# A third Strassen-like group of seven products in five blocks of each FFN, sums written over their own weights, and another order at the borders

## The chip, the core and the metric

The kernel runs on one core of a Trainium2 chip. The metric is the device time of one execution in microseconds. TensorE (PE) multiplies, PEld loads its stationary operand, VectorE (DVE) does elementwise work on two tensors, ScalarE (ACT) copies, scales and evaluates functions, SyncE (SP) issues nearly all DMAs. Each engine takes its own instructions in order and waits on semaphores for the others.

## What is computed

One decoder layer on 256 tokens of width 2048, all in float32:

```python
h = h + 0.5 * rms_norm(swiglu(rms_norm(h, pre1), gate1, up1, down1), post1)     # FFN 1, D_FF = 5632
h = h + rms_norm(hybrid_mixer(rms_norm(h, preM), ...) @ w_out, postM)           # GLA and MoBA heads
h = h + 0.5 * rms_norm(swiglu(rms_norm(h, pre2), gate2, up2, down2), post2)     # FFN 2
def swiglu(h, w_gate, w_up, w_down): return (silu(h @ w_gate) * (h @ w_up)) @ w_down
```

The weights are 352.67 MB, read once; each is used for 256 tokens, in two halves t of 128.

## The kernel before

**Precision.** A float32 product is made of three: every operand is split into a high part (rounded to fp32r) and a low part (the rest), and hi x hi, hi x lo and lo x hi are added in PSUM. Weights arrive in half MBs (`raw`, 128 x 1024: two k-tiles by 512 columns). `split` makes `whi` on ACT (L133) and `wlo` on DVE (L134). A ring of `RING = 8` pairs (hi, lo) stands between them and PE, and a ring of `RAW = 5` raw halves between the loads and the split. Each ordinary half is used by 12 matmuls of 512 columns (`mmt`, L320 to L322): two k-tiles, two token halves, three products.

**Order.** The weights' order is planned first (`plan...`, list `forms`). `take` hands the next split pair to PE, `done` gives it back, and both call `ahead`, which writes out loads while fewer than 5 raw halves are held and splits while fewer than 8 pairs are. Tile's scheduler then sets the order of each engine's instructions: ready work may be moved ahead of work that is written earlier but waits. On the chip that order is fixed.

**FFN.** 11 blocks of 512 gate and 512 up columns: blocks 0 and 1 plain (`up`, `columns`), blocks 2 to 10 mixed (`unit`). After block 2, half a down group (8 halves, `down`) stands before each mixed block; then come groups 4 and 5, the last in `down_last`. A mixed block treats the two token halves and two halves of a part of k as a 2 x 2 block matrix, as it does gate and up, and makes seven products for eight (`product`, L510 to L512, 6 matmuls each). One "group" ("q") covers four halves of weights (w11 and w12 of gate and up, w22, w21) and needs seven split pieces: w11, t1, t3, w22, t2, w21, t4, where t1 = w11 + w12, t2 = t1 + w22, t3 = w12 + w22 and t4 = t2 + w21 are sums on DVE (L139, L171) into a tile of their own. The rest of k goes as ordinary halves ("s"), 4 between and 4 after the two groups. The input's mixtures, the left-hand sides, are made once per FFN by `mixed`, in steps between the products of blocks 0 and 1; `NQ` is the number of k pieces it provides for. After the last group of a block L541 to L545 add the products' results from PSUM, after its last ordinary halves L556 to L561 make silu(gate) x up, and `turned` (L594, L595) transposes and splits the result for `down`.

**Borders.** `down_last` finishes a sub-layer. It goes through the token halves t and in each through four groups of 512 columns: L394 adds the PSUM result to the earlier sum in `f`, L395 squares it on ACT with a running sum, L396 multiplies by the post-norm weight. Two groups share one PSUM tile (`pt`, 4 buffers of two banks each). `Late` continues: `after` makes the row norm (`rstd_tok`, L265 to L267, then `refined`, L255 to L258), `update` adds to h (L432) and squares the new h (L433) for the next norm, `chunk` transposes h (L443) and splits it into `xh`, the next sub-layer's input (L450 on ACT, L451 on DVE), between the first products of the next block in `columns`. `warm` has ACT load the table for the square root. The end of the kernel uses `write_out` (L628) in place of `Late`.

Of the kernel before, what the change touches and what calls it, by code (L numbers as in the profile page):

```python
# [10 lines left out]
F32 = mybir.dt.float32  # L11
# [6 lines left out]
P = 128  # L18
# [19 lines left out]
NQ = 2  # L38
# [15 lines left out]
UNIT = [("q", 0), ("s", 4), ("s", 12), ("s", 5), ("s", 13), ("q", 1), ("s", 6), ("s", 14), ("s", 7), ("s", 15)]  # L54
# [3 lines left out]
def layer(ctx, tc, xT, x, wn, wpo, cst, msk, bdec, wup, wglr, gu1, dn1, win, wo, gu2, dn2, out):  # L58
# [29 lines left out]
    def plan_up(gu, b):  # L88
# [5 lines left out]
        for kind, i in UNIT:  # L94
# [19 lines left out]
    raws, ready, sums = [], [], []  # L114
    read, used, freed = [0], [0], [0]
    sum_pool = [None]
# [20 lines left out]
    def added(name, a, b):  # L137
        t = sum_pool[0].tile([P, 1024], F32, name=name, tag="sum", bufs=2)
        V.tensor_tensor(t, a, b, ALU.add)  # L139
        sums.append(t)  # L140


    NEEDS = {"w": 1, "w11": 2, "t1": 3, "t3": 3, "w22": 3, "t2": 3, "w21": 4, "t4": 4}
    ENDS = {"w": 1, "w11": 1, "t1": 1, "t3": 2, "w22": 3, "t2": 3, "w21": 4, "t4": 4}

    def can_prep():
# [4 lines left out]
        return len(raws) >= r + NEEDS[kind] and (kind[0] != "t" and kind != "w11" or sum_pool[0] is not None)  # L151

    def prep(cuts=1):
        kind, r = forms[len(ready)]
        w = raws[r:r + 4]
        if kind == "w" or kind == "w11":
            if kind == "w11":
                added("t1", w[0], w[1])
            split(w[0], cuts)
        elif kind == "t1":  # L160
            added("t2", sums[-1], w[2])
            split(sums[-2])
        elif kind == "t3":
            added("t3", w[1], w[2])
            split(sums[-1])
        elif kind == "w22":
            split(w[2])
        elif kind == "t2":
            split(sums[-2])
        elif kind == "w21":  # L170
            V.tensor_tensor(sums[-2], sums[-2], w[3], ALU.add)  # L171
            split(w[3])
        else:
            split(sums[-2])
# [155 lines left out]
    def columns(p, late=None):  # L330
# [3 lines left out]
        if late is not None:  # L334
            lead = []
            for t in range(NT):
# [3 lines left out]
                for i in range(LEAD):  # L340
# [36 lines left out]
    def down_last(g, lhs, wpost, sq, late):  # L377
# [4 lines left out]
        warm(eps)  # L382
        slots = []
        for t in range(NT):
            for m in range(4):
                if m % 2 == 0:
                    pair = pt()
                p = pair[:, m % 2]
# [4 lines left out]
                d = f[:, m, t]  # L393
# [628 lines left out]
```

## Time and profile before

| | |
|---|---|
| time, median of 3 runs | 1860.88 us (1860.2 to 1861.45) |
| the profiled execution | 1861.03 us, span 1859.2 us |
| granted TensorE clock, mean | 0.996 |
| PE, PEld, DVE, ACT busy | 98%, 82%, 77%, 54% |
| matmuls | 8516 |
| read from HBM | 352.67 MB, 191 GB/s over the span |

FFN 1 takes the span up to about 705 us, the mixer up to about 1122, FFN 2 the rest. A matmul's recorded duration is longer than the time until the next one starts, since they are pipelined; the starts tell the rate. The same holds for DVE and ACT to a smaller degree.

### The profile page before, as it was taken

To read this page: it belongs to the slowest core of one execution; us is meant where nothing else is said; L and a number is where in the kernel's file an instruction comes from. 1 tells how busy PE (TensorE), PEld (TensorE's weight loads), DVE (VectorE), ACT (ScalarE), POOL (GpSimd) and SP (SyncE) were. 2 spreads that over 40 slices of the span, in tenths; PEclk is the share of its full clock that TensorE was granted. 3 is DMA by queue.
4 is the path that set the end of the run, shared out by engine and by line. 5 is a ranking of instruction groups with operands and counts; after the bars stand their busy time and mean duration, and the time that the engine had idled before them with its cause. 6 is when DMAs were issued, how large, how long until landed. Compare 5 with 4: busy or idle time off the path is not lost.

```text
span 1859.2 us, 22693 instructions
## 1 busy us (share of the span) xinstructions
PE 1830.4 (98%) x8516; PEld 1518.6 (82%) x8516; DVE 1428.9 (77%) x1568; ACT 999.8 (54%) x1191; POOL 0.2 (0%) x4
## 2 busy tenths in 40 slices
PE   8999999999999998999999998999999999999997
PEld 6888888888888886889888886888888888888886
DVE  6788888888888857568455648778888888888875
ACT  7555555455545546454445547545564555455552
POOL 0000000000000000000000000000000000000000
PEclk9999999999999999999999999999999999999999
DMA  8664666556555763644355553645665565556571
GB/s 331 215 215 159 200 221 211 172 192 228 192 191 194 247 206 111 231 150 142 131 169 171 200 184 110 221 168 193 226 202 177 198 227 174 201 203 215 171 249 67
DMA packets 99086, 356.27 MB, mean 192 GB/s; under 512 B 11136, under 2 KB 11392, under 8 KB 98720
## 3 DMA queue, kind: packets, MB, share of 16 engines
q1 hardware_dynamic: 98400, 353.77, 56.9%
q8 instruction: 67, 1.10, 0.2%
q10 hardware_dynamic: 576, 1.05, 0.2%
q14 instruction: 43, 0.35, 0.1%
HBM read 352.67 MB, written 2.10 MB: 191 GB/s over the span
## 4 chain that ended last, share of the span: by engine, by line
PE 97%; ACT 1%; DVE 1%; DMA 0%; issue 0%; DVEq 0%; SPq 0%; ACTq 0%
PE pt L320 22%; PE pt L321 22%; PE pt L322 22%; PE pt L308 6%; PE pt L510 6%; PE pt L511 6%; PE pt L512 6%; PE pt L309 3%; PE pt L588 1%; PE pt L804 1%; ACT whi L133 1%; DVE h L628 0%; DVE wlo L134 0%; ACT f L433 0%; DVE f L394 0%
## 5 line engine op out<-in xcount | busy, mean ns | idle before, releaser
L134 DVE TENSOR_TENSOR wlo<-raw,whi 128x1024 fp32r<-128x1024 f32 (+1 forms) x621 | 755.6, 1220 | 235.7 <-ACT whi L133 218.7
L133 ACT ACTIVATE whi<-raw 128x1024 fp32r<-128x1024 f32 (+1 forms) x621 | 655.6, 1058 | 474.9 <-PE pt L322 306.4
L320 PE MATMUL pt<-whi,xh 128*128 128x512 f32 x1088 | 429.1, 395 | 13.3 <-ACT whi L133 6.2
L322 PE MATMUL pt<-whi,xh 128*128 128x512 f32 x1088 | 425.6, 392 | 1.0 <-DVE rt_v L267 0.6
L321 PE MATMUL pt<-wlo,xh 128*128 128x512 f32 x1088 | 426.1, 392 | 0.0
L133 ACT ACTIVATE whi<-t 128x1024 fp32r<-128x1024 f32 x144 | 152.3, 1057 | 258.6 <-DVE t L139 155.0
L320 PE MATMUL pt<-whi,act 128*128 128x512 f32 x704 | 276.6, 393 | 3.7 <-DVE f L394 3.6
L321 PE MATMUL pt<-wlo,act 128*128 128x512 f32 x704 | 274.7, 390 | 0.0
L322 PE MATMUL pt<-whi,act 128*128 128x512 f32 x704 | 274.5, 390 | 0.0
L320 PEld LDWEIGHTS pt<-whi,xh 128*128 128x128 f32 x1088 | 205.2, 189 | 61.7 <-ACT xh L450 10.4
L322 PEld LDWEIGHTS pt<-whi,xh 128*128 128x128 f32 x1088 | 205.2, 189 | 46.6 <-DVE xh L451 2.5
L321 PEld LDWEIGHTS pt<-wlo,xh 128*128 128x128 f32 x1088 | 205.2, 189 | 42.0 <-DVE wlo L134 0.9
L134 DVE TENSOR_TENSOR wlo<-t,whi 128x1024 fp32r<-128x1024 f32 x144 | 176.1, 1223 | 80.4 <-ACT whi L133 79.8
L308 PE MATMUL pt<-xh,whi 128*128 128x512 f32 x512 | 181.9, 399 | 0.0
L320 PEld LDWEIGHTS pt<-whi,act 128*128 128x128 f32 x704 | 132.6, 188 | 32.9 <-DVE f L394 5.3
L322 PEld LDWEIGHTS pt<-whi,act 128*128 128x128 f32 x704 | 132.6, 188 | 27.7
L321 PEld LDWEIGHTS pt<-wlo,act 128*128 128x128 f32 x704 | 132.6, 188 | 26.8
L309 PE MATMUL pt<-xh,wlo 128*128 128x256 f32 x512 | 143.7, 281 | 0.0
L139 DVE TENSOR_TENSOR t<-raw 128x1024 f32<-128x1024 f32 x72 | 88.1, 1224 | 42.2 <-DMA raw<-in_gu 41.0
L308 PEld LDWEIGHTS pt<-xh,whi 128*128 128x128 f32 x512 | 96.1, 188 | 22.6 <-issue 0.8
L510 PE MATMUL pt<-whi,mix 128*128 128x512 f32 x288 | 112.0, 389 | 0.0
L511 PE MATMUL pt<-wlo,mix 128*128 128x512 f32 x288 | 112.0, 389 | 0.0
(175 smaller groups left out, 1618.7 us busy)
## 6 DMA issues: line engine op xcount, KB each, us to landing
raw<-in_gu SPq DMA_DIRECT2D x351, 512.0 KB, 4.0
raw<-in_dn SPq DMA_DIRECT2D x176, 512.0 KB, 4.6
raw<-in_win SPq DMA_DIRECT2D x96, 512.0 KB, 3.4
raw<-in_wo SPq DMA_DIRECT2D x32, 512.0 KB, 3.3
wpost<-in_wpo SPq DMA_DIRECT2D x6, 512.0 KB, 6.2
hT<-in_xT SPq DMA_DIRECT2D x8, 256.0 KB, 7.0
h<-in_x SPq DMA_DIRECT2D x2, 1024.0 KB, 9.4
out<-h SPq DMA_DIRECT2D x4, 256.0 KB, 2.6
```

The costliest lines, as they stand in the source:

```text
L133: A.activation(hi[:, c], w[:, c], AF.Copy)
L134: V.tensor_tensor(lo[:, c], w[:, c], hi[:, c].bitcast(F32), ALU.subtract)
L139: V.tensor_tensor(t, a, b, ALU.add)
L308: T.matmul(o, hv[:, k, c], a, start=first and k == 0, stop=False)
L309: T.matmul(o[:, S:], lv[:, k, c], a[:, 0:S], start=False, stop=last and k == 1)
L320: T.matmul(o, hi, hv[:, i], start=first and i == 0, stop=False)
L321: T.matmul(o, hi, lv[:, i], start=False, stop=False)
L322: T.matmul(o, lo, hv[:, i], start=False, stop=last and i == 1)
L510: T.matmul(o, a[:, 0], hv[:, i], start=first and i == 0, stop=False)
L511: T.matmul(o, a[:, 0], lv[:, i], start=False, stop=False)
L512: T.matmul(o, a[:, 1], hv[:, i], start=False, stop=last and i == 1)
L588: T.transpose(p[:, j // 2, j % 2 * S + t * P:j % 2 * S + (t + 1) * P], s[:, t, j * P:(j + 1) * P], ident)
```

## The change

- `NQ` becomes 3, and a mixed block has one of two orders: blocks 3, 5, 7, 9 and 10 three groups and 4 ordinary halves (2 after the first group, 2 at the end), the others two groups and 8 halves, as before.
- A group's sums are written over the raw halves: w11 + w12 over w11 once w11 is split, and so on. The pieces come in the order w11, t1, w22, t2, t3, w21, t4. The sum tiles go; raw halves are given back later (`ENDS`).
- `mixed` works in place on 12 k-tiles of the input in place of 8; the mixtures' last third lies in a new tile `mix2`.
- `down_last`: each result has a PSUM tile of its own; the sum goes to a separate tile, from which ACT squares and DVE multiplies; `warm` stands behind the second square of the first token half and reads its sum.
- `Late`: the squares of the new h and the row norm move from `update` to `norm`, called after the fifth weight of `columns` in each token half.

```diff
-NQ = 2
+NQ = 3
...
+UNITS = ([("q", 0), ("s", 2), ("s", 10), ("s", 5), ("s", 13), ("q", 1), ("s", 6), ("s", 14), ("s", 7), ("s", 15)],
+         [("q", 0), ("s", 6), ("s", 14), ("q", 1), ("q", 2), ("s", 7), ("s", 15)])
+def unit_of(b):
+    return UNITS[b in (3, 5, 7, 9, 10)]
...
-        forms.extend((kind, len(source)) for kind in ("w11", "t1", "t3", "w22", "t2", "w21", "t4"))
+        forms.extend((kind, len(source)) for kind in ("w11", "t1", "w22", "t2", "t3", "w21", "t4"))
...
-    NEEDS = {"w": 1, "w11": 2, "t1": 3, "t3": 3, "w22": 3, "t2": 3, "w21": 4, "t4": 4}
-    ENDS = {"w": 1, "w11": 1, "t1": 1, "t3": 2, "w22": 3, "t2": 3, "w21": 4, "t4": 4}
+    NEEDS = {"w": 1, "w11": 2, "t1": 2, "w22": 3, "t2": 3, "t3": 3, "w21": 4, "t4": 4}
+    ENDS = {"w": 1, "w11": 0, "t1": 0, "w22": 0, "t2": 1, "t3": 2, "w21": 2, "t4": 4}
...
-        if kind == "w" or kind == "w11":
-            if kind == "w11":
-                added("t1", w[0], w[1])
-            split(w[0], cuts)
-        elif kind == "t1":
-            added("t2", sums[-1], w[2])
-            split(sums[-2])
...
+        if kind == "t2":
+            V.tensor_tensor(w[2], w[0], w[2], ALU.add)
+        elif kind == "t4":
+            V.tensor_tensor(w[3], w[2], w[3], ALU.add)
+        split(w[{"w": 0, "w11": 0, "t1": 0, "w22": 2, "t2": 2, "t3": 1, "w21": 3, "t4": 3}[kind]], cuts)
+        if kind == "w11":
+            V.tensor_tensor(w[0], w[0], w[1], ALU.add)
         elif kind == "w22":
+            V.tensor_tensor(w[1], w[1], w[2], ALU.add)
...
+                    if i == 4:
+                        late.norm(t)
...
-        warm(eps)
         slots = []
         for t in range(NT):
             for m in range(4):
-                if m % 2 == 0:
-                    pair = pt()
-                p = pair[:, m % 2]
+                p = pt()[:, t]
...
-                d = f[:, m, t]
-                V.tensor_tensor(d, d, p, ALU.add)
+                d = sums_[m % 2]
+                V.tensor_tensor(d, f[:, m, t], p, ALU.add)
                 A.activation(sq, d, AF.Square, accum_out=ss[t][:, m:m + 1])
-                V.tensor_tensor(d, d, wpost[m // 2][:, m % 2], ALU.mult)
+                if t == 0 and m == 1:
+                    warm(ss[t][:, 0:1])
+                V.tensor_tensor(f[:, m, t], d, wpost[m // 2][:, m % 2], ALU.mult)
...
-                A.activation(f[:, m, t], c, AF.Square, accum_out=self.hs[t][:, m:m + 1])
+        def norm(self, t):
+            for m in range(4):
+                A.activation(f[:, m, t], h[:, t, m * 512:(m + 1) * 512], AF.Square, accum_out=self.hs[t][:, m:m + 1])
             self.rc[t] = rstd_tok(self.hs[t], D)
...
-            mix = [low.tile([P, 2, 2 * NQ, P], F32R, name="mix", tag="quad", bufs=4) for _ in range(4)]
+            mix = [low.tile([P, 2, 4, P], F32R, name="mix", tag="quad", bufs=4) for _ in range(4)]
+            mix2 = fp.tile([P, 4, 2, 2 * NQ - 4, P], F32R, name="mix2")
...
-                V.tensor_tensor(m[:, 0], x22, x21, ALU.subtract)
-                V.scalar_tensor_tensor(m[:, 1], m[:, 0], -1.0, x11, op0=ALU.mult, op1=ALU.subtract)
+                V.tensor_tensor(x22, x22, x21, ALU.subtract)
+                V.tensor_tensor(x21, x11, x21, ALU.subtract)
                 yield
-                V.tensor_tensor(m[:, 2], x11, x21, ALU.subtract)
-                V.tensor_tensor(m[:, 3], x12, m[:, 1], ALU.add)
-                for i in range(4):
+                V.scalar_tensor_tensor(x11, x22, -1.0, x11, op0=ALU.mult, op1=ALU.subtract)
+                V.tensor_tensor(x12, x12, x11, ALU.add)
+                for i, m in enumerate((x22, x11, x21, x12)):
                     if i % 2 == 0:
                         yield
-                    A.activation(mix[i][:, 0], m[:, i], AF.Copy)
-                    V.tensor_tensor(mix[i][:, 1], m[:, i], mix[i][:, 0].bitcast(F32), ALU.subtract)
+                    for d, c in ((mix[i], m[:, 0:4]), (mix2[:, i], m[:, 4:])):
+                        A.activation(d[:, 0], c, AF.Copy)
+                        V.tensor_tensor(d[:, 1], c, d[:, 0].bitcast(F32), ALU.subtract)
...
-                for kind, i in UNIT:
+                for kind, i in unit_of(b):
...
-                            product(o, take(), i, lhs, first(name), alone and nq == NQ)
+                            product(o, take(), i, lhs, first(name), alone and nq == quads)
```

## Rows read from the trace of the kernel before

**Rows 1.** The page: busy time and share of the engines, and VectorE's busy tenths in 40 slices of the span.

```profile
PE 1830.4 (98%) x8516; PEld 1518.6 (82%) x8516; DVE 1428.9 (77%) x1568; ACT 999.8 (54%) x1191; POOL 0.2 (0%) x4
...
DVE  6788888888888857568455648778888888888875
```

**Rows 2.** The page: the chain of work that ended last, share of the span by engine.

```profile
PE 97%; ACT 1%; DVE 1%; DMA 0%; issue 0%; DVEq 0%; SPq 0%; ACTq 0%
```

**Rows 3.** The waits of TensorE: what waited for what, us in total, times, longest us.

```profile
PE pt L320 <- DVE f L394: 5.9, 3, 2.3
PE pt L320 <- ACT xh L450: 4.6, 6, 1.5
```

**Rows 4.** Windows over the eight periods (half a down group and the next mixed block) around blocks 3 to 10 of FFN 1; first, last and sum. Columns: stretch and length, busy us (and instructions) of PE, PEld, DVE, ACT and POOL, granted clock, DMA share, GB/s.

```profile
150.10:213.55 63.45, 63.45 (x286) 52.65 (x285) 50.68 (x49) 35.04 (x36) 0.00 (x0) 1.00 0.60 199
...
594.31:657.78 63.47, 63.47 (x286) 52.65 (x285) 53.60 (x50) 36.87 (x37) 0.00 (x0) 1.00 0.65 218
sum 507.68, PE 507.68 PEld 421.18 DVE 430.17 ACT 276.76 POOL 0.00; mean PE 63.46 PEld 52.65 DVE 53.77 ACT 34.59 POOL 0.00
```

**Rows 5.** Timeline of TensorE inside block 3: start, duration, and what it is; every third matmul of a run.

```profile
176.79 0.39 PE L320 MATMUL pt<-whi,xh 128*128 128x512 f32 x1
...
177.47 0.39 PE L320 MATMUL pt<-whi,xh 128*128 128x512 f32 x1
```

**Rows 6.** Timeline of VectorE in the second group of block 3: start, duration, what it is, and in brackets the idle time before it with what ended it.

```profile
174.08 1.23 DVE L139 TENSOR_TENSOR t<-raw 128x1024 f32<-128x1024 f32 x1
176.52 1.22 DVE L134 TENSOR_TENSOR wlo<-t,whi 128x1024 fp32r<-128x1024 f32 x1 [1.21 <-ACT whi L133]
177.66 1.22 DVE L134 TENSOR_TENSOR wlo<-raw,whi 128x1024 fp32r<-128x1024 f32 x1
...
183.49 1.23 DVE L134 TENSOR_TENSOR wlo<-t,whi 128x1024 fp32r<-128x1024 f32 x1 [1.21 <-ACT whi L133]
```

**Rows 7.** Timeline of ScalarE in block 3: the first ordinary half after the first group, and the high part of t3 in the second group.

```profile
162.08 1.06 ACT L133 ACTIVATE whi<-raw 128x1024 fp32r<-128x1024 f32 x1 [1.38 <-PE pt L322]
...
175.42 1.06 ACT L133 ACTIVATE whi<-t 128x1024 fp32r<-128x1024 f32 x1 [4.58 <-DVE t L139]
```

**Rows 8.** Timeline of VectorE at the end of block 2: two additions of 512 columns in a row, and the block's last product of 1024.

```profile
142.50 0.68 DVE L557 TENSOR_TENSOR fu<-pt,fu 128x512 f32<-128x512 f32 x1
143.10 0.74 DVE L558 SCALAR_TENSOR_TENSOR fs<-pt,rho,fs 128x512 f32<-128x512 f32 x1
...
146.15 1.28 DVE L561 SCALAR_TENSOR_TENSOR fs<-fu,rs_c,fs 128x1024 f32<-128x1024 f32 x1
```

**Rows 9.** Timeline: the low part of block 3's first piece on VectorE, its first use on TensorE (hi x lo), and the use of the last piece of the block's second group.

```profile
145.01 1.22 DVE L134 TENSOR_TENSOR wlo<-raw,whi 128x1024 fp32r<-128x1024 f32 x1
...
162.05 0.39 PE L511 MATMUL pt<-wlo,xh 128*128 128x512 f32 x1
...
190.61 0.39 PE L511 MATMUL pt<-wlo,xh 128*128 128x512 f32 x1
```

**Rows 10.** Timeline of VectorE before block 4's first group: its first sum, and the low part of an ordinary half that is planned ahead of it.

```profile
203.67 1.23 DVE L139 TENSOR_TENSOR t<-raw 128x1024 f32<-128x1024 f32 x1 [3.57 <-DMA raw<-in_gu]
204.81 1.22 DVE L134 TENSOR_TENSOR wlo<-raw,whi 128x1024 fp32r<-128x1024 f32 x1
```

**Rows 11.** Timeline: the addition that frees the first PSUM pair of block 3 after its last group, and the first matmul of the down group behind the block.

```profile
191.51 0.68 DVE L542 TENSOR_TENSOR fs<-pt,fs 128x512 f32<-128x512 f32 x1
...
202.63 0.39 PE L320 MATMUL pt<-whi,act 128*128 128x512 f32 x1
```

**Rows 12.** Windows at the border between FFN 1 and the mixer (three), and at that between the mixer and FFN 2 (the last one); columns as in rows 4.

```profile
705.10:707.80 2.70, 0.45 (x2) 0.03 (x1) 2.48 (x6) 2.68 (x5) 0.00 (x0) 1.00 0.15 23
707.80:711.60 3.80, 3.74 (x10) 2.93 (x11) 3.70 (x11) 2.30 (x5) 0.00 (x0) 0.55 0.77 254
711.60:745.00 33.40, 30.21 (x138) 21.96 (x137) 28.15 (x69) 25.65 (x65) 0.00 (x0) 1.00 0.39 134
...
1128.10:1160.00 31.90, 29.38 (x134) 21.57 (x134) 28.38 (x71) 24.93 (x64) 0.00 (x0) 1.00 0.36 111
```

**Rows 13.** Timeline at the first border: TensorE's waits and its first transposes, and on ScalarE the square root's table and the first of four squares of the new h.

```profile
706.86 1.28 ACT L266 ACT_TABLE_LOAD   x1
708.16 0.29 ACT L266 ACTIVATE rt_s<-rt_q,eps 128x1 f32<-128x1 f32 x1
...
713.47 0.61 ACT L433 ACTIVATE f<-h 128x512 f32<-128x512 f32 x1
...
707.86 0.52 PE L320 MATMUL pt<-whi,act 128*128 128x512 f32 x1 [2.31 <-DVE f L394]
712.30 0.60 PE L443 MATMUL pt<-cs,h 128*128 128x128 f32 x4
717.12 0.50 PE L320 MATMUL pt<-whi,xh 128*128 128x512 f32 x1 [1.47 <-ACT xh L450]
```

**Rows 14.** Timeline at the end: TensorE's last wait, the additions to h of the first token half on VectorE, and the last multiplication by the post-norm weight.

```profile
1846.47 0.50 PE L320 MATMUL pt<-whi,act 128*128 128x512 f32 x1 [1.30 <-DVE f L394]
...
1842.48 2.73 DVE L628 SCALAR_TENSOR_TENSOR h<-f,rs_c,h 128x512 f32<-128x512 f32 x4
...
1851.05 0.69 DVE L396 TENSOR_TENSOR f<-f,wpost 128x512 f32<-128x512 f32 x1 [0.85 <-ACT fu L395]
```

**Rows 15.** The page: DMA issues; line, engine and operation, count, KB each, median us from issue to landing.

```profile
raw<-in_gu SPq DMA_DIRECT2D x351, 512.0 KB, 4.0
```

More of the change, by code (lines that the diff above doesn't have):

```diff
@@ L112, in layer @@
     plan_ffn(gu2, dn2)
-    raws, ready, sums = [], [], []
+    raws, ready = [], []
     read, used, freed = [0], [0], [0]
-    sum_pool = [None]
     def load(cuts=1):
@@ L135, in split @@
         ready.append((hi, lo))
[L137 to L140, printed above, removed]
-    NEEDS = {"w": 1, "w11": 2, "t1": 3, "t3": 3, "w22": 3, "t2": 3, "w21": 4, "t4": 4}
-    ENDS = {"w": 1, "w11": 1, "t1": 1, "t3": 2, "w22": 3, "t2": 3, "w21": 4, "t4": 4}
+    NEEDS = {"w": 1, "w11": 2, "t1": 2, "w22": 3, "t2": 3, "t3": 3, "w21": 4, "t4": 4}
+    ENDS = {"w": 1, "w11": 0, "t1": 0, "w22": 0, "t2": 1, "t3": 2, "w21": 2, "t4": 4}
     def can_prep():
@@ L150, in can_prep @@
         kind, r = forms[i]
-        return len(raws) >= r + NEEDS[kind] and (kind[0] != "t" and kind != "w11" or sum_pool[0] is not None)
+        return len(raws) >= r + NEEDS[kind]
     def prep(cuts=1):
@@ L375, in down, with down_last @@
                 V.tensor_tensor(f[:, m], f[:, m], p, ALU.add)
-    def down_last(g, lhs, wpost, sq, late):
+    def down_last(g, lhs, wpost, sums_, sq, late):
         a, b = g
         n = (b - a) // 2
-        warm(eps)
         slots = []
@@ L405, in down_last, with split2 @@
                 late.after(t, ss[t])
+    def split2(x):
+        return [x[:, 0], x[:, 1]]
     class Late:
@@ L523, in unit @@
                 nq, ns = 0, 0
+                quads = sum(kind == "q" for kind, i in unit_of(b))
+                slots = len(unit_of(b)) - quads
                 begun = set()
@@ L529, in first @@
                     return new
-                for kind, i in UNIT:
+                for kind, i in unit_of(b):
                     if kind == "q":
@@ L549, in unit @@
                         j, k = i // 8, 2 * (i % 8)
-                        end = ns > 2 * (8 - 2 * NQ) - 2
+                        end = ns > slots - 2
                         mmt(p23[:, j], 0, slot, (k, k + 1), first(("w21", "w22")[j]), end, xrhs)
@@ L553, in unit @@
                         done()
-                        if nq == NQ:
+                        if nq == quads:
                             step()
@@ L605, in ffn @@
                 elif kind == "down":
-                    down_last(DOWN_FFN[i], arhs, wpost, fp.tile([P, NT, 512], F32, name="fu")[:, 0], next_)
+                    down_last(DOWN_FFN[i], arhs, wpost, split2(fp.tile([P, NT, 512], F32, name="fu")),
+                              fp.tile([P, NT, 512], F32, name="fs", bufs=2)[:, 0], next_)
                 else:
@@ L612, in ffn @@
                         post_weight(wpost[i], post, scale, i)
-            sum_pool[0] = None
     class WriteOut:
@@ L950, in layer @@
         down(DOWN_MIX[0], range(4), xrhs)
-        sq = tmp.tile([P, 2, S], F32, name="tb").rearrange("p a s -> p (a s)")
-        down_last(DOWN_MIX[1], xrhs, wpost, sq, ffn2_in)
+        row = lambda name: tmp.tile([P, 2, S], F32, name=name).rearrange("p a s -> p (a s)")
+        down_last(DOWN_MIX[1], xrhs, wpost, [row("bt"), row("bt")], row("tb"), ffn2_in)
     ffn(ffn2_in, False, 2, 0.5, WriteOut())
```

18 lines of the change are left out of this document (2 added, 16 removed).

## The prediction

> **What bounds the kernel now.** I read the shares of the engines first: TensorE (PE) is busy 98% of the 1859.2 us span, VectorE (DVE) 77%, and DVE's slices stand at 8 tenths through both FFNs [rows 1]. The chain that ended last is 97% PE [rows 2], so time is won in two ways only: fewer matmuls, or less waiting of PE. Its list of waits is short: 5.9 us for the additions of L394 in three places and 4.6 us for the high parts of the normed input in six [rows 3]; both belong to the borders between the sub-layers. Inside an FFN a period of half a down group and one mixed block repeats every 63.45 us with PE busy throughout, while DVE works 53.8 us of it on average [rows 4]. So within the FFNs matmuls are the price, and DVE is the engine that could take over.
>
> **The products.** Three matmuls start in 0.68 us [rows 5], so one takes 0.227 us at full clock, a product (6) 1.36 us, a group of seven 9.52 us, and an ordinary half MB (12 matmuls) 2.72 us. A block with two groups has 14 x 6 + 8 x 12 = 180 matmuls, with three 21 x 6 + 4 x 12 = 174. Five blocks of each FFN change: 10 x 1.36 = **13.6 us** less on PE.
>
> **What DVE pays for it.** A third group turns 4 halves into 7 split pieces and adds four sums: 7 operations of 1024 columns per changed block. Back to back these start 1.14 us apart (176.52, 177.66), though each is recorded with 1.22 [rows 6]; so 8.0 us per block. Over the eight periods of blocks 3 to 10 DVE's 430.2 us become 430.2 + 5 x 8.0 = 470.1, PE's 507.7 become 500.9 [rows 4]: 30.8 us of DVE room for 21 groups, 1.47 us each.
>
> The page "VectorE: DVE Perf Modes" of the Trainium skill, section "The DRAIN you can't avoid", says that the next operation doesn't issue until the pipe is empty. By that each would cost its 1.22 us, DVE would need about 470 x 1.22 / 1.14 = 503 us, and five blocks would not fit; the starts 1.14 apart speak against it, and the sum goes by them.
>
> **The waits inside a group.** That room matters because DVE takes its instructions in order. Where a sum is split at once, DVE adds, ScalarE (ACT) makes the high part, DVE subtracts: sum at 174.08, high part at 175.42, low part at 176.52 [rows 6, 7]. That is 2.44 us from start to start where 1.14 would do: 1.30 us of DVE are lost. The old group has one such place, the sum for t3. With sums written over their half MBs there are three, since the sum must follow the split of the raw half: t1, t2 and t4. The old sums could run early (the one at 203.67 goes ahead of pieces that wait for their slots [rows 10]); of the new ones only the sum for t3 can. It needs the first sum and the third half MB, so it can fill t1's wait (1.14 of 1.30). Between t2 and t4 I let one be filled by the block's other DVE work (0.60 us each, 1.28 for the last product [rows 8]) or by t3's ready piece, and count n = 1 lost wait per group; the bounds are 0 and 3.
>
> **The lead.** A group costs DVE 11 x 1.14 + 1.30n = 12.5 + 1.3n against PE's 9.52, so the lead of the finished pieces over their use shrinks by 3.0 + 1.3n; an ordinary half gives back 2.72 - 1.14 = 1.58. A block begins with 15.8 us (low part done at 146.23, used at 162.05) and its last group ends with 5.9 (184.72, 190.61) [rows 6, 9]. The eight slots cap it: the high part at 162.08 waited for PE [rows 7]. The cap is the PE time of the seven slots between, less some 2.4 us for the split: 7.1 after a group, 9.8 after a group and two halves. A three-group block thus comes out of its first group at 7.1 for any n up to 3, has 9.8 before the second, and loses 2 x (3.0 + 1.3n): +3.8, +1.2, -1.4, -4.0 us for n = 0, 1, 2, 3. Then come ten ordinary halves and 8 transposes, 28.1 us of PE, against 21.0 us of DVE (11.4 of splits, 9.6 of additions and products by rows 8): +7.1. A two-group block goes +6.3 between its groups and +10.3 after. Run through blocks 3 to 10 with these steps, n = 1 gives a shortfall only in block 10, which follows block 9 directly (8.3 - 4.3 + 3.2 - 8.6 = -1.4): 1.4 per FFN, **+3 us**. n = 2 gives 1.4 in four blocks and 6.5 in block 10, 12 per FFN, +24 us; n = 3 gives 37 per FFN, +74 us; n = 0 nothing.
>
> **At nothing.** The larger mixed input (one more 1024 and one more 512 addition, four operations half as long again, four extra splits) is about 4.2 us of DVE by rows 6 and 8; it lies under blocks 0 and 1, where DVE is 6 and 7 tenths busy [rows 1], some 28 us idle; without that cover it is 4.2 us per FFN. Raw halves are held longer, so loads start later; one lands in 4.0 us [rows 15]. Where group follows group, SP can load the next group's third half when t3's low part is done; its first reader comes five operations and a lost wait later, 5 x 1.14 + 1.30 = 7.0 us, so 3 us are to spare. A late one would hold DVE's whole queue behind it.
>
> **The borders.** Before, two 512-wide results share a PSUM pair, and PE doesn't begin the second until DVE has taken the first: it stands 2.31 us until 707.86 [rows 13], and then runs about 3.4 us at half clock (granted mean 0.55 over 3.80 us, the 1.2 GHz level), which loses 1.7 [rows 12]. With a fresh pair for each result both go: 2.25 + 1.7, and the second border has the same wait in rows 3, together 7.9. The four squares of the new input, 0.61 us each from 713.47 on ACT, stand ahead of the high parts for which PE waits 1.47 us until 717.12 [rows 13]; moved behind them, 1.47 at each border, 2.9 together, of the 3.19 and 2.52 us that PE idles in those stretches [rows 12]. At the end 1.30 us of waiting for L394 behind four L628, and 0.85 that the last multiplication waits for ACT [rows 14]: 2.2. Total **13.0 us**. What is late next is the row norm of the first half: its chain reaches PE with the transposes at 712.30 [rows 13], and PE will be there about 4 us sooner; the earlier Sqrt table (1.28 us on ACT [rows 13]) and a multiplication that no longer waits pay for part of that. Bounds: 0, if the chain gives it all back, and 17, if all idling of rows 12 and 14 goes.
>
> "ScalarE: Activation LUTs" of the Trainium skill, section "What ACT_TABLE_LOAD costs", gives 1283 ns and about 1380 ns of draining behind each. By that taking the load off three chains would be worth about 4 us more; here the root starts at 708.16, 0.02 us after the load ends [rows 13], so I count 1.28 only, and inside the 13.0.
>
> **Sum.** The profiled execution took 1861.03 us, 0.1 above the median of 1860.88, so no correction is needed: 1861.0 - 13.6 - 13.0 + 3 = 1837.4, say **1838 us**.
>
> **Rivals.**
> (a) Two lost waits per group: +24 instead of +3, 1859 us. For it: the split pieces keep one order in the group shown. Against: t1's filler depends on little.
> (b) The other side: all three waits stay lost in every group, +74, **1909 us**. DVE sets the pace of the blocks and its queue holds back the epilogues too. For it: in [rows 6, 7] ACT sat 4.58 us before t3's high part while the raw half due next, which the sum at 174.08 itself reads, had landed, and it kept its order. It turns the change into a loss from a shortfall of 26.6 us, a little above n = 2.
> (c) The result pairs come free late. After the last group only two halves, not four, stand before the next down group needs a pair: 1.36 + 5.44 = 6.8 us. The addition that frees it stands behind seven splits, 7 x 1.14 + 0.6 = 8.6 us. Now it is done by 192.2 and needed at 202.63 [rows 11]. The price is 1.8 us less the lead, 0.6 to 1.8 in ten blocks: 6 to 18 us, 1844 to 1856.
> (d) The borders don't do what they say: PE meets the norm's chain instead of L394, and the clock falls again after that wait. 1838 + 13 = 1851 us.
>
> **How the numbers follow.** Forecast 0.54, (a) 0.14, (b) 0.10, (c) 0.10, (d) 0.12. About 0.2%, 3.7 us, is what a measurement of this kernel tells from no change. Forecast, (c) and (d) are faster, (a) lies across the line (a third faster, half the same, the rest slower); with a few parts in a hundred moved from (c) and (d) for two of them together: faster 0.76, same 0.08, slower 0.16. The range runs from 1828 (n = 0 and the upper bound at the borders, 1861 - 13.6 - 17 = 1830, less 0.1% because the stretches of rows 12 end where I cut them) to 1872, which takes in (a) with two-thirds of (c) on top and leaves out (b); the forecast's own range is 1828 to 1846.
>
> **What would show it.** Right: 60 fewer matmuls; PE busy through the 62.1 us periods; DVE near 94% in blocks 3 to 10; no PE wait for L394 and no half clock near 708 and 1124; at most one ACT-ended gap of 1.2 us per group on DVE. Wrong: PE waits for high or low parts in second and third groups, growing to block 10 (a, b); for L542's buffer at the first down product (c); or for high parts behind L432 at the borders (d). The term that would make it wrong is n.

## The result: slower by 1.5%, where 1.2% faster was forecast

The changed kernel takes 1887.57 us (median; 1885.95 to 1891.43) against 1861.06 us before, a ratio of 1.0146 with a 95% interval of 1.0129 to 1.0164. The forecast was 1838 us with a range up to 1872. The profiled execution took 1886.35 us with a span of 1884.6 us, 25.4 more than the 1859.2 before. Its mean granted clock was 0.998, against 0.996 before, so the clock isn't what was lost in it: the time went into waiting.

The page of the changed kernel: busy time of the engines and the chain that ended last.

```profile
PE 1827.7 (97%) x8456; PEld 1503.7 (80%) x8456; DVE 1512.4 (80%) x1650; ACT 1021.6 (54%) x1229; POOL 0.2 (0%) x4
```

```profile
PE 65%; DVE 21%; issue 5%; ACT 5%; DMA 4%; SPq 0%; ACTq 0%; DVEq 0%
```

TensorE has 60 matmuls fewer, as counted [rows 1]. But the chain, 97% TensorE before [rows 2], is now TensorE for 65% and VectorE for 21%: stretches of the FFNs run at VectorE's pace. The page's busy time of TensorE hardly moves (1830.4 to 1827.7): a matmul that starts after a wait is recorded longer, 0.50 us where 0.39 is usual.

The waits of TensorE in the changed kernel (what waited for what, us in total, times, longest us). The lines have moved: L138 and L139 are the high and low parts (L133, L134 before), L508 to L510 a product, L311 to L313 `mmt`, L588 a block's transposes, L441 those of h.

```profile
PE pt L508 <- ACT whi L138: 16.9, 21, 1.5
PE pt L311 <- ACT whi L138: 10.6, 11, 6.1
PE pt L588 <- DVE fs L561: 6.9, 9, 1.3
PE pt L441 <- DVE h L427: 4.6, 2, 2.3
PE pt L509 <- DVE wlo L139: 3.4, 6, 0.8
```

Two of these rows answer to [rows 3]: the wait for L394 is gone, and one for h, 2.3 us at each of two borders, has come. The others are new and lie in the FFNs, except 6.1 of L311's at the kernel's start, which was there before. Where they lie is seen best in two long windows (stretch, length, busy us and instructions of PE, PEld, DVE, ACT, POOL, clock, DMA share, GB/s), the changed kernel first, then the kernel before:

```profile
160.00:690.00 530.00, 513.60 (x2264) 418.00 (x2263) 469.69 (x439) 287.06 (x295) 0.00 (x0) 1.00 0.57 198
```

```profile
160.00:690.00 530.00, 530.00 (x2372) 439.67 (x2371) 440.62 (x412) 284.31 (x286) 0.00 (x0) 1.00 0.61 204
```

In the same 530 us TensorE starts 108 instructions fewer, at full clock. At the old pace of 530 / 2372 = 0.223 us these are 24 us. Summed over all starts in the trace (each interval between neighbours beyond the regular one of 0.227 us, or 0.11 for a transpose), TensorE loses 24.6 us in FFN 1 and 24.7 in FFN 2, where the kernel before lost 0.07 and 0.12. The two borders fall from 11.2 and 10.2 to 6.9 each, the end from 2.2 to 0. So the account closes: -13.6 + 49 - 10 = +25, against +25.4 in the spans. Of the 49, waits for pieces and the slower starts right behind them are 37, the waits for L561 8.4, and one stretch at half clock late in FFN 2 (granted 0.50 over 3.41 us from 1801.25) 1.7; the other 2 are spread over many starts.

TensorE in block 3's third group and before the block's transposes (start, duration, what, idle time before it and what ended it):

```profile
196.20 0.50 PE L508 MATMUL pt<-whi,xh 128*128 128x512 f32 x1 [1.17 <-ACT whi L138]
...
216.00 1.10 PE L588 MATMUL pt<-cs,fs 128*128 128x128 f32 x8 [0.96 <-DVE fs L561]
```

The first is a piece that comes late, the second is the block's result behind the pieces. In FFN 1 block 3 loses 2.8 and 1.1 us in these two ways, block 9 3.7 and 0.6, block 10 5.6 and 1.1: the pattern that the prediction had named for its rivals (a) and (b), waits in second and third groups, largest in block 10.

VectorE's timeline points to the cause. The second group of block 3 in the changed kernel, up to the first sum of the third (L163 is t1's sum, L165 t3's, L157 t2's, L159 t4's; "x2" are two operations, the first duration covers both):

```profile
166.89 1.22 DVE L163 TENSOR_TENSOR raw<-raw 128x1024 f32<-128x1024 f32 x1
168.15 1.22 DVE L165 TENSOR_TENSOR raw<-raw 128x1024 f32<-128x1024 f32 x1
169.32 2.36 DVE L139 TENSOR_TENSOR wlo<-raw,whi 128x1024 fp32r<-128x1024 f32 x2
171.72 1.23 DVE L157 TENSOR_TENSOR raw<-raw 128x1024 f32<-128x1024 f32 x1
174.15 3.50 DVE L139 TENSOR_TENSOR wlo<-raw,whi 128x1024 fp32r<-128x1024 f32 x3 [1.21 <-ACT whi L138]
177.68 1.22 DVE L159 TENSOR_TENSOR raw<-raw 128x1024 f32<-128x1024 f32 x1
180.11 2.36 DVE L139 TENSOR_TENSOR wlo<-raw,whi 128x1024 fp32r<-128x1024 f32 x2 [1.21 <-ACT whi L138]
182.51 1.22 DVE L163 TENSOR_TENSOR raw<-raw 128x1024 f32<-128x1024 f32 x1
```

From t1's sum to the next one (166.89 to 182.51) a group takes 15.62 us of VectorE. Eleven operations at 1.14 are 12.54. Two waits of 1.21, behind the sums of t2 and of t4, cost 1.30 each. And each of the four sums starts 1.26 us after the operation before it where 1.14 is usual; each writes over what that operation reads. 12.54 + 2 x 1.30 + 4 x 0.12 = 15.62. TensorE uses a group's seven pieces in 9.52, so the lead shrinks by 6.1 us per group; with n = 1 the prediction had 4.3.

Not every group is like this one. Over blocks 3 to 10 of FFN 1, 30 of the 42 waits behind the sums of t2 and t4 stand idle for 1.2 us. In the second groups of all five three-group blocks both do. In the third groups only t2's does, since L543 and L544 run behind t4's sum; but t4's low part comes no sooner for it (193.78 to 196.24 in block 3, 2.46 us). In some first groups L595 fills part of t2's.

### The profile page after: what moved, and what is told of

Read it like the earlier page. It is cut to its first block, busy times and chain, and to the rows that moved or that the text cites. A ratio compares the mean times of both kernels' runs of the same rounds, so it can differ in the third digit from the quotient of the medians.

```text
span 1884.6 us, 22728 instructions
## 1 busy us (share of the span) xinstructions
PE 1827.7 (97%) x8456; PEld 1503.7 (80%) x8456; DVE 1512.4 (80%) x1650; ACT 1021.6 (54%) x1229; POOL 0.2 (0%) x4
## 4 chain that ended last, share of the span: by engine, by line
PE 65%; DVE 21%; issue 5%; ACT 5%; DMA 4%; SPq 0%; ACTq 0%; DVEq 0%
PE pt L311 14%; PE pt L313 14%; PE pt L312 14%; DVE wlo L139 12%; PE pt L299 6%; ACT whi L138 4%; PE pt L300 3%; PE pt L510 3%; PE pt L509 3%; PE pt L508 3%; DMA raw<-in_dn 3%; DVE raw L163 1%; DVE raw L157 1%; DVE raw L165 1%; DVE raw L159 1%
## 5 line engine op out<-in xcount | busy, mean ns | idle before, releaser
L138 ACT ACTIVATE whi<-raw 128x1024 fp32r<-128x1024 f32 (+1 forms) x795 | 816.4, 1055 | 711.5 <-PE pt L313 166.9
L139 DVE TENSOR_TENSOR wlo<-raw,whi 128x1024 fp32r<-128x1024 f32 (+1 forms) x795 | 945.0, 1219 | 310.7 <-ACT whi L138 308.2
L311 PE MATMUL pt<-whi,xh 128*128 128x512 f32 x928 | 366.9, 395 | 12.1 <-ACT whi L138 10.6
L313 PE MATMUL pt<-whi,xh 128*128 128x512 f32 x928 | 363.2, 392 | 1.9 <-DVE rt_v L258 1.2
L312 PE MATMUL pt<-wlo,xh 128*128 128x512 f32 x928 | 362.9, 391 | 0.5 <-DVE wlo L139 0.5
L311 PE MATMUL pt<-whi,act 128*128 128x512 f32 x704 | 275.8, 392 | 0.0
L313 PE MATMUL pt<-whi,act 128*128 128x512 f32 x704 | 274.1, 389 | 0.0
L311 PEld LDWEIGHTS pt<-whi,xh 128*128 128x128 f32 x928 | 174.9, 188 | 54.7 <-ACT whi L138 13.7
L313 PEld LDWEIGHTS pt<-whi,xh 128*128 128x128 f32 x928 | 174.6, 188 | 41.1 <-DVE xh L449 2.9
L312 PEld LDWEIGHTS pt<-wlo,xh 128*128 128x128 f32 x928 | 174.9, 188 | 36.7 <-DVE wlo L139 1.4
L313 PEld LDWEIGHTS pt<-whi,act 128*128 128x128 f32 x704 | 132.2, 188 | 27.6
L311 PEld LDWEIGHTS pt<-whi,act 128*128 128x128 f32 x704 | 132.2, 188 | 26.7
L508 PE MATMUL pt<-whi,mix 128*128 128x512 f32 x368 | 144.8, 393 | 6.3 <-ACT whi L138 6.3
L509 PE MATMUL pt<-wlo,mix 128*128 128x512 f32 x368 | 144.8, 393 | 3.4 <-DVE wlo L139 3.4
L510 PE MATMUL pt<-whi,mix 128*128 128x512 f32 x368 | 143.5, 390 | 0.0
L508 PE MATMUL pt<-whi,xh 128*128 128x512 f32 x276 | 108.8, 394 | 10.6 <-ACT whi L138 10.6
L509 PE MATMUL pt<-wlo,xh 128*128 128x512 f32 x276 | 108.8, 394 | 0.0
```

The costliest lines, as they stand in the source:

```text
L138: A.activation(hi[:, c], w[:, c], AF.Copy)
L139: V.tensor_tensor(lo[:, c], w[:, c], hi[:, c].bitcast(F32), ALU.subtract)
L311: T.matmul(o, hi, hv[:, i], start=first and i == 0, stop=False)
L312: T.matmul(o, hi, lv[:, i], start=False, stop=False)
L313: T.matmul(o, lo, hv[:, i], start=False, stop=last and i == 1)
L508: T.matmul(o, a[:, 0], hv[:, i], start=first and i == 0, stop=False)
```

## The experiments

Two theories stood against each other. W: the places where VectorE waits for ScalarE inside a group set the length of a group, and that makes the loss. R: the sums over the raw halves hold these longer, so loads come late. A third, C, is that a three-group block is simply too much VectorE work, waits or not. The borders were taken apart beside them. The code cuts show the lines that matter, not each line that follows from them.

**The borders alone.** The kernel before with `down_last`, `norm` and the new place of `warm`, nothing else:

```diff
-                if m % 2 == 0:
-                    pair = pt()
-                p = pair[:, m % 2]
+                p = pt()[:, t]
...
-                d = f[:, m, t]
-                V.tensor_tensor(d, d, p, ALU.add)
+                d = sums_[m % 2]
+                V.tensor_tensor(d, f[:, m, t], p, ALU.add)
```

> The kernel before with the border edits alone (own PSUM tile per result, separate sum tile, later Sqrt table, squares and row norm moved): two groups per mixed block, sums in their own tiles. Theory W (the lost time lies in waits inside the groups of the mixed blocks; the borders gain about 10 us in the trace of the changed kernel): 1851 us, with a TensorE wait for the updated h of about 2.5 us at each border. If the borders gain nothing (rival d): 1861 us. If they gain all that was forecast: 1848 us.

Measured: 1853.07 us, ratio 0.9961 (0.9946 to 0.9976). About 7 us of the 13.0 came. TensorE's wait; the stretches right behind it at both borders (columns as above); and the first operation of the row norm and the first additions to h at the first border:

```profile
PE pt L450 <- DVE h L436: 4.6, 2, 2.3
```

```profile
709.66:714.10 4.44, 4.44 (x15) 3.59 (x16) 4.13 (x7) 3.60 (x11) 0.00 (x0) 0.62 0.24 90
1123.58:1128.00 4.42, 4.42 (x15) 3.67 (x16) 3.93 (x6) 3.06 (x10) 0.00 (x0) 0.61 0.23 87
```

```profile
703.57 0.16 DVE L265 TENSOR_REDUCE rt_q<-ss 128x1 f32<-128x4 f32 x1
...
708.86 2.73 DVE L436 SCALAR_TENSOR_TENSOR h<-f,rs_c,h 128x512 f32<-128x512 f32 x4
```

TensorE's new wait ends at 709.66 and 1123.58, and behind each the clock falls again: granted 0.50 for 3.41 us, 1.7 lost. That is rival (d) in full, wait and clock. The row norm is six operations of 0.15 us on VectorE and a root on ScalarE, yet from L265 to the first addition to h it takes 5.3 us, where it took 3.1 before (707.07 to 710.18): weight splits and the next results' additions stand between its operations in VectorE's queue.

**The norm taken out of that.** The same kernel, with a constant in place of the post-norm's row scale (this scale is left out of the result):

```diff
-            self.r[t] = rstd_tok(ss, D)
+            self.r[t] = eps
```

> The kernel before with the new borders alone, and in it the post-norm's row scale of the additions to h replaced by a constant that is ready from the start: the sums, the root and the small VectorE operations of that norm are left out (the output lacks this scale; everything else stays). Theory H (the row norm's chain, some 5 us from the last square to the first addition to h, is what TensorE's two waits of 2.3 us before the transposes of h end on): the additions to h can start at about 703.5, well ahead of the transposes at 707.4, so both waits go, 1853 becomes 1848 to 1849. Rival Q (VectorE's queue at the border is late by itself, with weight splits and the next results' additions): the waits stay, or others of the same size take their place, 1851 to 1853.

Measured: 1845.33 us, ratio 0.9914 (0.9899 to 0.9928). No wait for h is left, and the addition to h stands right behind its factor:

```profile
702.88 0.69 DVE L397 TENSOR_TENSOR f<-fu,wpost 128x512 f32<-128x512 f32 x1
703.61 0.75 DVE L436 SCALAR_TENSOR_TENSOR h<-f,eps,h 128x512 f32<-128x512 f32 x1
```

So the norm's chain is what holds the new borders, for 7.7 us, more than the 4.6 of the wait itself: the borders' losses fall from 8.1 and 8.6 to 5.0 and 3.7, since the two stretches at half clock, 3.4 us together, go with it. The run takes the whole chain out; how much of its length is VectorE's queue and how much the operations themselves it doesn't separate.

**Two groups everywhere.** The change with sums in place and the new borders, but no third group:

```diff
-    return UNITS[b in (3, 5, 7, 9, 10)]
+    return UNITS[0]
```

> The changed kernel with two groups in every mixed block: sums over their own half MBs and the border edits stay, the third groups go. Theory W: the two lost VectorE waits per group (15.6 us per group in place of 12.5) still fit under TensorE's 63.45 us periods, so 1851 us, the same as the border edits alone, and no TensorE wait in the mixed blocks. Theory R (raw halves are held too long and loads come late): some of the 49 us of waits stays, above 1856 us.

Measured: 1853.33 us, ratio 0.9961 (0.9946 to 0.9976), the time of the borders alone, though the second group of each of blocks 3 to 10 has the same two waits of 1.21 us. With two groups there is room for them. Loads do come later, so that ScalarE waits for halves of the down weights 64 times (38.1 us) where it was 22 times (13.4 us) in the kernel before, but TensorE waits for none of it: in-place sums and late returns of raw halves cost no time by themselves.

**Three groups with the old sums.** The change with the sums in tiles of their own, the old order and the old, earlier return of raw halves (only the order is shown):

```diff
-        forms.extend((kind, len(source)) for kind in ("w11", "t1", "w22", "t2", "t3", "w21", "t4"))
+        forms.extend((kind, len(source)) for kind in ("w11", "t1", "t3", "w22", "t2", "w21", "t4"))
```

> The changed kernel (three groups in blocks 3, 5, 7, 9, 10, border edits) with the sums in tiles of their own and the pieces in the old order, raw halves given back as before. Theory W: the old order also loses a wait at t3 and, in some groups, one at t4, but none of the 0.1 us steps between dependent sums; between 1 and 2 lost waits per group give 3 to 24 us of waiting in both FFNs, so 1841 to 1862 us, and if it has close to 2 the upper end. Theory R: loads are early again, 1838 us. Theory C (VectorE's bare work is too much for three groups, whatever the order): 1880 us or more.

Measured: 1857.45 us, ratio 0.9985 (0.9976 to 0.9995). VectorE in block 3, where one group follows another (L140 low part, L146 and L178 sums):

```profile
168.32 1.22 DVE L146 TENSOR_TENSOR t<-raw 128x1024 f32<-128x1024 f32 x1
170.75 1.23 DVE L140 TENSOR_TENSOR wlo<-t,whi 128x1024 fp32r<-128x1024 f32 x1 [1.21 <-ACT whi L139]
...
175.30 1.22 DVE L178 TENSOR_TENSOR t<-t,raw 128x1024 f32<-128x1024 f32 x1
176.44 1.22 DVE L146 TENSOR_TENSOR t<-raw 128x1024 f32<-128x1024 f32 x1
177.73 1.23 DVE L140 TENSOR_TENSOR wlo<-t,whi 128x1024 fp32r<-128x1024 f32 x1
...
182.40 1.22 DVE L146 TENSOR_TENSOR t<-raw 128x1024 f32<-128x1024 f32 x1
```

Where group follows group there is one wait: the next group's first sum, at 176.44, fills t4's. In the block's last group t4's stays too (1.21 us until 191.81). A group is 14.08 us (168.32 to 182.40), and TensorE loses 9.1 and 8.2 us in the FFNs. This is close to the prediction's n = 1, in another kernel than the one that was forecast, and it still isn't the +3 us that the prediction had for it. The waits for pieces lie in block 10 alone, as its ledger said, about 3 us per FFN where it had 1.4; the larger part are the waits before the transposes of block results, which it didn't have (L605 is the transposes, L578 the block's last product):

```profile
PE pt L605 <- DVE fs L578: 6.7, 10, 1.0
```

**No waits.** In place, with an order that lets splits of other pieces stand between a sum and its reader:

```diff
-        forms.extend((kind, len(source)) for kind in ("w11", "t1", "w22", "t2", "t3", "w21", "t4"))
+        forms.extend((kind, len(source)) for kind in ("w11", "w22", "t1", "w21", "t3", "t2", "t4"))
...
-        if kind == "t2":
+        split(w[{"w": 0, "w11": 0, "t1": 0, "w22": 2, "t2": 2, "t3": 1, "w21": 3, "t4": 3}[kind]], cuts)
+        if kind == "w22":
+            V.tensor_tensor(w[0], w[0], w[1], ALU.add)
+            V.tensor_tensor(w[1], w[1], w[2], ALU.add)
             V.tensor_tensor(w[2], w[0], w[2], ALU.add)
-        elif kind == "t4":
+        elif kind == "w21":
             V.tensor_tensor(w[3], w[2], w[3], ALU.add)
-        split(w[{"w": 0, "w11": 0, "t1": 0, "w22": 2, "t2": 2, "t3": 1, "w21": 3, "t4": 3}[kind]], cuts)
-
-        if kind == "w11":
-            V.tensor_tensor(w[0], w[0], w[1], ALU.add)
-        elif kind == "w22":
-            V.tensor_tensor(w[1], w[1], w[2], ALU.add)
```

> The changed kernel with the pieces in another order, w11, w22, t1, w21, t3, t2, t4, and each sum written at least one piece ahead of its own split (three sums behind the split of w22, the fourth behind that of w21); sums stay over their own half MBs, raw halves are given back as late or later. Theory W: the 1.2 us gaps on VectorE inside the groups go, a group takes about 13 us in place of 15.6, nearly all of the 49 us of waits in the FFNs goes, 1836 to 1842 us. Theory C: 1880 us or more. Theory R: no gain, since the halves are held as long, 1885 us.

Measured: 1845.25 us, ratio 0.9919 (0.9904 to 0.9933), faster than both kernels. VectorE in block 3 (L158, L159, L160, L162 the sums of t1, t3, t2, t4):

```profile
167.77 1.22 DVE L158 TENSOR_TENSOR raw<-raw 128x1024 f32<-128x1024 f32 x1
169.03 1.23 DVE L159 TENSOR_TENSOR raw<-raw 128x1024 f32<-128x1024 f32 x1
170.20 1.23 DVE L139 TENSOR_TENSOR wlo<-raw,whi 128x1024 fp32r<-128x1024 f32 x1
171.35 1.22 DVE L160 TENSOR_TENSOR raw<-raw 128x1024 f32<-128x1024 f32 x1
172.48 2.35 DVE L139 TENSOR_TENSOR wlo<-raw,whi 128x1024 fp32r<-128x1024 f32 x2
174.75 1.22 DVE L162 TENSOR_TENSOR raw<-raw 128x1024 f32<-128x1024 f32 x1
175.89 4.79 DVE L139 TENSOR_TENSOR wlo<-raw,whi 128x1024 fp32r<-128x1024 f32 x4
180.59 1.22 DVE L158 TENSOR_TENSOR raw<-raw 128x1024 f32<-128x1024 f32 x1
```

No gap over 0.1 us, and 12.82 us per group (167.77 to 180.59). TensorE's loss in the FFNs falls from 49 to 5.6 us (3.4 and 2.2) with the same number of operations on VectorE, and with raw halves held as long. R and C fall for this block pattern, W stands: VectorE's work was not too much, its waits were. Three of the four sums also start 1.14 us after the operation before them, no longer 1.26, which is some 0.35 of the 2.8 us that a group got shorter.

**Half of it.** Only t2's sum moved, behind w22's split, with t3's piece written ahead of t2's:

```diff
-        forms.extend((kind, len(source)) for kind in ("w11", "t1", "w22", "t2", "t3", "w21", "t4"))
+        forms.extend((kind, len(source)) for kind in ("w11", "t1", "w22", "t3", "t2", "w21", "t4"))
...
-        if kind == "t2":
-            V.tensor_tensor(w[2], w[0], w[2], ALU.add)
-        elif kind == "t4":
+        if kind == "t4":
...
             V.tensor_tensor(w[1], w[1], w[2], ALU.add)
+            V.tensor_tensor(w[2], w[0], w[2], ALU.add)
```

> The changed kernel with t3 ahead of t2 (w11, t1, w22, t3, t2, w21, t4) and t2's sum behind the split of w22, so that t3's piece lies between t2's sum and its split; t4's sum stays next to its split. Theory W: one lost wait of 1.3 us per group in place of two, a group of about 14.2 us between 15.6 (the change) and 12.8 (the order filled throughout); by the ledger of leads only block 10 falls short, 7 us in both FFNs over the filled order: 1849 to 1856 us. If the two waits cost in proportion: halfway, 1866 us.

Measured: 1882.88 us, ratio 1.0122 (1.0107 to 1.0137), a miss as an experiment. VectorE's order shows why (L164 is t2's sum):

```profile
169.63 3.50 DVE L139 TENSOR_TENSOR wlo<-raw,whi 128x1024 fp32r<-128x1024 f32 x3
173.04 1.22 DVE L164 TENSOR_TENSOR raw<-raw 128x1024 f32<-128x1024 f32 x1
175.47 2.36 DVE L139 TENSOR_TENSOR wlo<-raw,whi 128x1024 fp32r<-128x1024 f32 x2 [1.21 <-ACT whi L138]
```

t3's piece is one of the three at 169.63, ahead of the sum that it was to cover. The scheduler moved the ready piece forward, and the wait stayed. t4's stays too, so that both waits are still in the group, and the time stays within 0.3% of the change: that fits W, but tells nothing on the size of one wait.

**Later transposes.** The change, with `turned` of a three-group block two matmul steps later:

```diff
-                yield from idle(3)
+                yield from idle(5 if b in (3, 5, 7, 9, 10) else 3)
```

> The changed kernel with the transposes of a three-group block's result (line 588) two slots later. Its own waits for the block's last product sum to 8.4 us in the trace of the changed kernel. If they are a cost of their own: 1879 us. Theory W (VectorE is late as a whole, and the wait only shows where PE meets it): PE waits elsewhere for as long, 1884 to 1888 us.

Measured: 1883.4 us, ratio 1.0124 (1.0102 to 1.0146). The 6.9 us of waits for L561 are gone. TensorE's waits for pieces:

```profile
PE pt L508 <- ACT whi L138: 13.6, 16, 1.2
PE pt L311 <- ACT whi L138: 10.6, 11, 6.2
PE pt L509 <- DVE wlo L139: 4.9, 8, 0.8
```

They don't take the place of the others: these three rows sum to 29.1 us, in the changed kernel to 30.9. What took it in this trace is the clock. Six stretches of 3.41 us in its FFNs, each behind waits for pieces, were granted 0.50, where the changed kernel's trace has one; six lose 10 us. One of them:

```profile
456.32:459.73 3.41, 3.41 (x10) 2.63 (x9) 3.41 (x4) 2.56 (x3) 0.00 (x0) 0.50 0.86 247
```

So the time doesn't decide between the two expectations. The executions of this kernel range from 1879.09 us, at a mean granted clock of 0.996, to 1888.2 at 0.990, and the waits in the trace speak for the first: the wait before the transposes was a cost of its own.

**The same in the good order.** The order of pieces without waits, and the edit just shown:

```diff
-                yield from idle(3)
+                yield from idle(5 if b in (3, 5, 7, 9, 10) else 3)
```

> The order of pieces that lets other splits stand between a sum and its readers, with the transposes of a three-group block two matmul steps of the down group later. With this order VectorE has nearly a product's room per group, so the waits of TensorE before L585's counterpart (2.3 us in three places) can go without coming back elsewhere: FFN loss 5.5 becomes about 2.5, 1845.3 becomes 1842 to 1843. Rival: VectorE is late there anyway, as in the change with the same later transposes, and the time stays at 1845.

Measured: 1841.15 us, ratio 0.9893 (0.9877 to 0.991), the fastest of all. The FFNs' loss is 1.2 and 1.3 us, spread over many starts: no wait of TensorE is left in blocks 3 to 10, and none has come elsewhere. VectorE is busy 480.80 of 530 us, TensorE all of them:

```profile
160.00:690.00 530.00, 530.00 (x2368) 438.66 (x2367) 480.80 (x451) 301.78 (x305) 0.00 (x0) 1.00 0.62 207
```

**The transposes of h one result later as well.** To the kernel just told:

```diff
-                    if m in (1, 2):
-                        late.early(m - 1)
+                    if m in (2, 3):
+                        late.early(m - 2)
```

> The filled order, with the early transposes of the new h at the borders one result later (behind the third and fourth result of the second token half) and the later transposes of a three-group block's result. The filled order measured 1845 us; its trace has TensorE waiting 2.5 us for the updated h at each of two borders and 3 us for the last product before the transposes of block results. If both go and nothing takes their place: 1837 us. If TensorE then waits for the high parts of the input instead: 1842 us.

Measured: 1845.33 us, ratio 0.9919 (0.9904 to 0.9934), no gain. The wait for h, 4.6 us, turned into two of 1.4 us for results that VectorE adds late (L381). That alone would be shorter. But in this trace the first border has 6.83 us at half clock (from 711.47), where the kernel just told has 3.41; neither has any at the second. That is 1.7 us, as much as the shorter waits gave back. This execution is 1.8 us longer than that of the kernel just told, the median 4.2; where the rest went these runs don't settle.

**Three groups in all nine blocks.** The good order and the later transposes of h, but `idle(3)`, with 24 matmuls fewer per FFN than with five such blocks:

```diff
-    return UNITS[b in (3, 5, 7, 9, 10)]
+    return UNITS[1]
```

> The filled order with three groups in all nine mixed blocks of each FFN, and the later early transposes at the borders (not the later transposes of block results). TensorE does 8 x 1.36 = 11 us less than with five. VectorE's work per period is then 61.8 us of 62.1. By the ledger of leads a group of 12.8 us costs 3.3 us of lead, a block ends with 3.2 us and starts with 10.3, so no group falls short: 1830 to 1838 us. If VectorE's bare work is the limit (theory C): above 1845 us.

Measured: 1849.45 us, ratio 0.9943 (0.9929 to 0.9958), a miss. TensorE has 11 us less to do and waits more. Its longest wait, VectorE's load, and the page's chain that ended last:

```profile
PE pt L585 <- DVE fs L558: 7.6, 8, 1.7
```

```profile
160.00:690.00 530.00, 526.57 (x2342) 433.52 (x2342) 500.81 (x473) 308.69 (x313) 0.00 (x0) 1.00 0.61 207
```

```profile
PE 39%; DVE 35%; DMA 13%; issue 9%; ACT 4%; DVEq 0%; ACTq 0%; SPq 0%
```

VectorE is at 500.81 of 530 us, 94%, and the FFNs lose 6.9 and 9.3 us, with 3.1 more before block 3. That is what theory C expects, but it isn't shown. Hardly a group has a wait for ScalarE left, yet DMA is 13% of the chain, and ScalarE waits 118 us for raw halves (81 in the filled order), so late loads are a rival. And the 7.6 us are the waits that later transposes removed with five such blocks; that edit wasn't tried here.

## Why the prediction was wrong, step by step

- **The products: right.** 60 matmuls fewer, 13.6 us. The fastest version shows it: 1861.0 - 13.6 - 7 for the borders + 2.5 for the FFNs' rest = 1843, measured 1841.
- **VectorE's work: right.** The page has 82 operations more. In a group they start 1.14 apart, save where one writes over what the one before it reads (1.26), 0.5 us per group that the sum lacked. The Trainium skill's "VectorE: DVE Perf Modes", section "The DRAIN you can't avoid", which the prediction set against the rows, also says that an operation which isn't held starts earlier; that sentence agrees with the 1.14.
- **n = 1: the step that failed.** The mechanism was the right one, and so was t1's wait filled by t3's sum (166.89, 168.15). But the prediction let one of t2's and t4's waits be filled "by the block's other DVE work or by t3's ready piece". t3's low part stands behind t2's in VectorE's order (the three operations at 174.15 are t2, t3 and w21), so it fills nothing. The block's other work fills some waits in first groups and t4's in third groups, where it brings no piece forward. In the second groups, with which the lead begins to be lost, n was 2 in all five three-group blocks of FFN 1, and t4 came as late in the third. The sign hung on this term.
- **The rows of before told it.** The prediction wrote that the old group has one such place. The rows themselves [rows 6] have two lost waits, at 176.52 and at 183.49: the second is t4's, which was put down to nothing. The trace of before has it, 1.21 us each time, in the second group of every block from 3 to 10 of FFN 1. Had both been counted, the old order would have stood as evidence that t4's wait isn't filled, and n = 2 would have been the likeliest.
- **The ledger of leads: right in form, and steep.** With 6.1 us lost per group (n = 2 and the four starts at 1.26) it gives, as an estimate, a shortfall of 2.4 us in block 3, 3.6 in each of 5, 7 and 9, and 8.0 in block 10: 21 per FFN, 42 in all. The waits for pieces measure 37; block 10's are 5.6 and not 8.0. The prediction's own price of n = 2, 24 us, was for 5.6 per group; half a microsecond per group makes 42 of it, since a block has no lead left beyond that point.
- **The waits before the transposes: a term that the prediction lacked.** The waits for L561 are 8.4 us in the changed kernel, and the larger part of the loss in the run with the old sums. In the good order the later transposes removed them, with nothing in their place. So n alone isn't the whole miss: rival (a) had the right mechanism at 1859, and the 28 us from there to 1886 (the profiled execution) are about 13 in the waits for pieces (37 for 24), 8 in these waits, 3 at the borders, 2 of clock and 2 spread. With n near 1 (the run with the old sums, 1857.45) the forecast of 1838 would still have missed.
- **At nothing: nearly right.** Loads do come later: ScalarE waits for halves of the down weights 102 times, 64.4 us in all, where it was 22 times and 13.4 before, and the page's chain has 4% DMA. But in the good order, where ScalarE still waits 86 times, 48.0 us, TensorE loses almost nothing, so this isn't what made the change slow. (c), the late pair of PSUM, wasn't seen: L542 begins at 193.18 and the next down group at 204.00.
- **The borders: 13.0 forecast, about 7 alone and 10 in the profiled execution of the change.** The waits for L394 went, and the 2.2 us at the end. But the row norm of the first token half, named as late next, took back 2.3 us of waiting at each border, and in the run with the borders alone the half clock came back behind both waits, all of rival (d)'s mechanism at half its price. In the changed kernel's profile the clock stayed full behind the same waits. With the same borders the other traces have half clock behind none of them, one or both, so 3 us of the 10 went with the execution and not with the edit. The earlier table load and the independent multiplication didn't shorten the norm's chain, which grew from 3.1 to 5.3 us; its six operations of 0.15 stand apart in VectorE's queue.

## What to carry to other kernels

Where an engine that works near its limit hands a piece to another and takes it back, count the hand-over and not only the operations: here a sum that is split at once costs 2.44 us of VectorE instead of 1.14, and an order that puts other splits between the two was worth 42 us with the same operations. Before costing a new order, mark every gap of the old order in its timeline and say for each who fills it. A ledger of leads is worth making, but near its turning point it must be run for the neighbouring values of each term, since there half a microsecond per group took its loss from 24 to 42 us. Before an edit is judged by a few microseconds, compare the granted clock of the two traces: here it hid what one experiment had gained.

## What the hardware showed beyond that

- The same pause of TensorE did and didn't cost the clock. Before, it idled 2.31 us until 707.86 and was granted 0.55 over the next 3.8 us [rows 12, 13]. With the borders alone it idles 2.30 us at both borders and falls to half clock behind both. In the changed kernel it idles 2.30 us until 727.20 (and until 1140.08), and the stretch behind it has the full clock. In the fastest version the same pause costs it at the first border and not at the second, in one execution. What differs isn't settled by these runs. The changed kernel's first border, the pause and what follows, then the fastest version's two stretches behind the pause:

```profile
724.90:727.20 2.30, 0.00 (x0) 0.00 (x1) 2.30 (x7) 1.92 (x5) 0.00 (x0) 1.00 0.71 216
727.20:731.00 3.80, 3.80 (x19) 3.22 (x20) 3.80 (x6) 3.80 (x12) 0.00 (x0) 1.00 0.28 111
```

```profile
704.02:708.40 4.38, 4.38 (x15) 3.68 (x16) 3.93 (x6) 3.06 (x10) 0.00 (x0) 0.62 0.19 76
1118.80:1123.20 4.40, 4.40 (x22) 3.70 (x23) 4.40 (x8) 4.40 (x12) 0.00 (x0) 1.00 0.22 81
```

- An operation of VectorE of 1024 columns that overwrites what the operation just before it reads starts 1.26 us after it, an independent one 1.14.
